# Gate products of a PEER block: the place of their PSUM columns turned round

## Chip, cores and metric

The kernel runs on one core of a Trainium2 chip. The metric is the device time of one execution in microseconds; less is better.

## The reference

Two transformer blocks run one after the other on 256 tokens of width 1024. The first has a short convolution, a latent attention and two SwiGLU layers, the second a chunked attention, an mLSTM and, as its feed-forward part, a PEER layer with 128 x 128 = 16384 experts. Only that layer is touched here:

```python
s_top, i_top = lax.top_k(s, PEER_TOPK)          # 8 heads, two key halves, 16 of 128 each
...
best, ci = lax.top_k(cand, PEER_TOPK)           # 16 of the 16 x 16 sums
e = i1 * N_KEYS + i2
gate = jax.nn.softmax(best, axis=-1)
u = u_exp[e]
v = v_exp[e]
act = jax.nn.gelu(jnp.einsum("thkd,td->thk", u, xb))
return jnp.einsum("thk,thkd->td", (gate * act).astype(xb.dtype), v)
```

Each token has 8 x 16 = 128 chosen experts, each with a gate.

## The kernel before

The kernel gathers no experts. It computes the activation of all 16384 experts for all 256 tokens, multiplies each by the gate (zero where an expert isn't chosen), and sums over all experts. Each fp32 product is made of three products of halves that the faster fp32 format holds (`whi`, `wlo`: high and low half of a weight; `pTh`, `pTl`: of the activations).

- `u_pair(c)` (L1411) takes the c-th of 64 chunks of `peer_u` (1 MB, two rows of 128 experts). ScalarE makes the high half, VectorE the low half (L128, L129), TensorE does 48 products of 256 columns into a bank, and ScalarE writes their GELU to the stash `ST[0]` (chunks 0 to 31) or `ST[1]` (32 to 63) (L1418). A stash holds, for each of 128 partitions (the second key), 64 first keys x 256 tokens in fp32: token neighbours token.
- `weights8(half, t0)` (L1537) makes the gates of 8 tokens and 64 first keys. VectorE compares the indices of the chosen experts with 0 to 127 (`B`, L1551, the second key) and with the 64 first keys of this half (`E`, L1552), and multiplies `E` by the gates, which are cut into three bf16 parts (`Aw`, three instructions of L1555). All of this is in the tile `one`, of which there are 2. For each token TensorE loads `B` (128 choices x 128 second keys) and streams `Aw` (128 choices x 64 first keys), three times, once for each part, into the same 64 columns of a bank: 24 products, each with its weight load. The bank is one of 2 with the tag `mb`. VectorE then multiplies the stash by the bank in place (L1562).
- `v_half` (L1571) multiplies the finished stash, cut into halves by `split` (L135), by the rows of `peer_v`: 12 products of 512 columns for each half chunk, into four banks `acc` that collect over the whole layer.

The order: u chunks 0 to 31; `weights8(0, ...)` for the 32 groups of 8 tokens, among the u chunks 32 to 62; u chunk 63; `weights8(1, ...)` for 32 groups, among the v chunks 0 to 31; v chunks 32 to 63; then residual and final norm. A planner that simulates the engines sets each engine's order; `prio(LOW)` (L1577, L1590) puts the groups behind the chunks, and `prio(-2 * LOW)` (L1557) puts their matmuls ahead of the chunks' again, so that TensorE does them as soon as the masks are planned to be ready. In the order that results, the products of two groups mostly stand together. SP issues the chunks' loads in the order of the code.

Of the kernel before, what the change touches and what calls it, by code (L numbers as in the profile page):

```python
# [16 lines left out]
ALU = mybir.AluOpType  # L17
# [44 lines left out]
def tile_kernel(ctx, tc, A, out, taps=None):  # L62
    nc = tc.nc
# [16 lines left out]
    def mmps(side=None):  # L80

        if side is None:
            turn[0] += 1
            side = turn[0] % turn[1] == 0
        if side:
            return psum.tile([P, 512], F32, name="mb", tag="mb", bufs=2)
        return psum.tile([P, 512], F32, name="mm", tag="mm", bufs=6)
# [4 lines left out]
    @contextmanager  # L92
    def prio(d):

        p = tc.cur_priority
        tc.cur_priority = max(0, p + d)
        try:
            yield
        finally:
            tc.cur_priority = p  # L100
# [44 lines left out]
    def mm(ps, lhsT, rhs, start, stop):  # L145
        nc.tensor.matmul(ps, lhsT, rhs, start=start, stop=stop, skip_group_check=True)  # L146
# [1250 lines left out]
    for c in range(3, 8):  # L1397
        hs = weights[c - 3] if c < 5 else q_halves(c)
        ps = mmps()
# [137 lines left out]
    def weights8(half, t0):  # L1537
        ps = mmps(True)
        n = 8
        one = pk.tile([P, n * 384], BF, name="one", tag="one", bufs=2)  # L1540
        B = one[:, :n * P].rearrange("p (t j) -> p t j", t=n)
        E = one[:, n * P:n * 192]
        Aw = one[:, n * 192:].rearrange("p (i t j) -> p i t j", i=3, t=n)

        def pairs(v, j):
            return v.rearrange("p (t j d) -> p t j d", t=n, d=2) if j is None else v.rearrange("p (j d) -> p j d", d=2)[:, None].to_broadcast([P, n, j, 2])

        def each(v, j):
            return v[:, t0:t0 + n, None, :].to_broadcast([P, n, j, 2])

        nc.vector.tensor_tensor(pairs(one[:, :n * P], None), pairs(iob, 64), each(iT[:, 1], 64), op=ALU.is_equal)  # L1551
        nc.vector.tensor_tensor(pairs(E, None), pairs(iob[:, half * 64:(half + 1) * 64], 32), each(iT[:, 0], 32), op=ALU.is_equal)  # L1552
        for i in range(3):
            o = n * 192 + i * n * 64
            nc.vector.tensor_tensor(pairs(one[:, o:o + n * 64], None), pairs(E, None), each(g3[:, i], 32), op=ALU.mult)  # L1555
        po = ps.rearrange("p (i t) -> p i t", t=n)
        with prio(-2 * LOW):  # L1557
            for t in range(n):
                for i in range(3):
                    mm(po[:, :, t], B[:, t, :], Aw[:, i, t, :], i == 0, i == 2)  # L1560
        v = ST[half][:, :, t0:t0 + n]
        nc.vector.tensor_tensor(v, po, v, op=ALU.mult)  # L1562

    def v_split(c):
        half, o = c // 32, (2 * c) % 64
# [11 lines left out]
    with prio(LOW):  # L1577
        for t0 in range(0, T, 8):
            weights8(0, t0)
# [10 lines left out]
    with prio(LOW):  # L1590
        for t0 in range(0, T, 8):
            weights8(1, t0)
# [31 lines left out]
    for tt in range(NT):  # L1624
        ss = ev[:, 6 * D + 8 * tt:6 * D + 8 * tt + 2]
        for j in range(2):
            o = slice(j * 512, (j + 1) * 512)
            t = rt[tt][:, o]
# [102 lines left out]
```

## Time and profile before

| | us |
|---|---|
| median of 3 runs | 1662.21 (1661.76 to 1663.13) |
| profiled execution | 1662.13 |
| its span, first to last instruction | 1660.4 |
| TensorE (PE) busy | 1637.8 (99%) |
| TensorE weight loads (PEld) | 1515.3 (91%) |
| VectorE (DVE) busy | 1183.4 (71%) |
| ScalarE (ACT) busy | 770.5 (46%) |
| POOL busy | 62.7 (4%) |
| 1536 gate products, sum of their durations | 98.1 |
| 64 products with the stash (L1562), busy time on VectorE | 41.3 |

The granted clock of TensorE is 0.999 of full speed over the span. Matmuls overlap: the sum of their durations is more than the time that they take up, and a start-to-start distance is read from the timeline. Each matmul has two instructions, the load of its stationary operand (PEld) and the product (PE). A line like L146 is that of a helper; tiles tell the groups apart: `mb<-one` are the gate products, `mm<-pT.,w..` the u chunks, `acc<-w..,pT.` the v chunks. The idle time in a group is that of the engine just before its instructions, with what ended it.

### The profile page before, as it was taken

Reading aid. Unit: us, or ns where it says so; the run is one execution under the profiler, and the core shown is the slowest. Engines: PE = TensorE matmul, PEld = TensorE weight load, DVE = VectorE, ACT = ScalarE, POOL = GpSimd, SP = SyncE. Lnnn points to the kernel's source line nnn. Section 1 sums busy time; section 2 is a strip of 40 time slices with the busy share of each in tenths; the row PEclk is TensorE's granted clock in tenths of the full one; section 3 lists DMA queues with packets and bytes.
Section 4 is the critical chain, followed back from the end, with each engine's and each line's share of the span. In section 5 each row is a group of like instructions: output and inputs, shape, how many; then the busy total and the mean of one; then the engine's idle time right before and its main releaser. Section 6 shows DMA issues by size and latency. Waiting matters only on the chain.

```text
span 1660.4 us, 28789 instructions
## 1 busy us (share of the span) xinstructions
PE 1637.8 (99%) x12006; PEld 1515.3 (91%) x12006; DVE 1183.4 (71%) x1925; ACT 770.5 (46%) x1064; POOL 62.7 (4%) x114
## 2 busy tenths in 40 slices
PE   7999999999999999999999999999999999999997
PEld 7999999989999899998999999999999888888886
DVE  5768776666878676766799984877747888755555
ACT  5545444464544466653544444333344333454443
POOL 0000000200000010002000000000000000000001
PEclk9999999999999999999999999999999999999999
DMA  5739665235866455463535545344355434455553
GB/s 225 283 135 349 261 258 220 94 132 218 339 256 242 178 170 176 144 247 130 194 128 180 184 170 181 128 142 137 128 183 212 165 135 155 159 188 201 186 195 127
DMA packets 46274, 312.76 MB, mean 188 GB/s; under 512 B 6240, under 2 KB 6256, under 8 KB 10304
## 3 DMA queue, kind: packets, MB, share of 16 engines
q1 hardware_dynamic: 43344, 300.82, 50.7%
q0 software_dynamic: 2656, 9.06, 1.6%
q8 instruction: 94, 1.54, 0.4%
q10 hardware_dynamic: 144, 1.05, 0.2%
q14 instruction: 36, 0.29, 0.1%
HBM read 308.78 MB, written 2.12 MB: 187 GB/s over the span
## 4 chain that ended last, share of the span: by engine, by line
PE 95%; DVE 2%; DMA 1%; ACT 1%; POOL 0%; issue 0%; SPq 0%; POOLq 0%; DVEq 0%; ACTq 0%
PE mm L146 46%; PE acc L146 32%; PE mb L146 16%; PE mm L217 0%; DMA raw<-in_conv_w_in 0%; DMA raw<-in_mla_w_uq 0%; POOL xn L1219 0%; DVE wlo L129 0%; DVE first L135 0%; ACT pTh L135 0%; PE mb L217 0%; DVE stash L1629 0%; DVE stash L1630 0%; DVE xn L1230 0%; DVE hres L1217 0%
## 5 line engine op out<-in xcount | busy, mean ns | idle before, releaser
L129 DVE TENSOR_TENSOR wlo<-raw,whi 128x1024 fp32r<-128x1024 f32 x492 | 597.7, 1223 | 278.9 <-ACT whi L128 277.8
L128 ACT ACTIVATE whi<-raw 128x1024 fp32r<-128x1024 f32 x492 | 514.6, 1057 | 602.2 <-PE mm L146 360.5
L146 PE MATMUL mm<-pTh,whi 128*128 128x256 f32 x1720 | 489.0, 284 | 0.0
L146 PE MATMUL mm<-pTl,whi 128*128 128x256 f32 x1720 | 487.9, 284 | 0.0
L146 PE MATMUL mm<-pTh,wlo 128*128 128x256 f32 x1720 | 487.2, 284 | 0.0
L146 PEld LDWEIGHTS mm<-pTh,whi 128*128 128x128 f32 x1720 | 329.7, 192 | 1.5 <-issue 0.3
L146 PEld LDWEIGHTS mm<-pTl,whi 128*128 128x128 f32 x1720 | 329.9, 192 | 0.8
L146 PEld LDWEIGHTS mm<-pTh,wlo 128*128 128x128 f32 x1720 | 329.5, 192 | 0.5
L146 PE MATMUL acc<-wlo,pTh 128*128 128x512 f32 x512 | 159.4, 391 | 0.0
L146 PE MATMUL acc<-whi,pTl 128*128 128x512 f32 x512 | 158.3, 389 | 0.0
L146 PE MATMUL acc<-whi,pTh 128*128 128x512 f32 x512 | 145.1, 391 | 0.0
L146 PEld LDWEIGHTS acc<-whi,pTl 128*128 128x128 f32 x512 | 96.1, 188 | 20.1
L146 PEld LDWEIGHTS acc<-whi,pTh 128*128 128x128 f32 x512 | 96.2, 188 | 19.6
L146 PEld LDWEIGHTS acc<-wlo,pTh 128*128 128x128 f32 x512 | 95.6, 189 | 19.1
L146 PE MATMUL mb<-pTh,whi 128*128 128x256 f32 x392 | 111.2, 284 | 0.0
L146 PE MATMUL mb<-pTh,wlo 128*128 128x256 f32 x392 | 110.9, 283 | 0.0
L146 PE MATMUL mb<-pTl,whi 128*128 128x256 f32 x392 | 110.9, 283 | 0.0
L146 PE MATMUL mb<-one 128*128 128x64 bf16 x1536 | 98.1, 246 | 0.0
L146 PEld LDWEIGHTS <-one 128*128 128x128 bf16 x1536 | 87.4, 123 | 6.8 <-DVE wlo L129 2.9
L135 ACT ACTIVATE pTh<-stash 128x512 fp32r<-128x512 f32 x64 | 40.6, 634 | 90.6 <-PE acc L146 89.0
L146 PEld LDWEIGHTS mb<-pTh,whi 128*128 128x128 f32 x392 | 74.8, 191 | 0.6
L146 PEld LDWEIGHTS mb<-pTl,whi 128*128 128x128 f32 x392 | 74.8, 191 | 0.5
(533 smaller groups left out, 2141.5 us busy)
## 6 DMA issues: line engine op xcount, KB each, us to landing
raw<-in_peer_u SPq DMA_DIRECT2D x64, 1024.0 KB, 4.8
raw<-in_peer_v SPq DMA_DIRECT2D x64, 1024.0 KB, 4.8
raw<-in_conv_ffn_w SPq DMA_DIRECT2D x33, 1024.0 KB, 6.8
raw<-in_mla_ffn_w SPq DMA_DIRECT2D x33, 1024.0 KB, 6.8
raw<-in_w_ada SPq DMA_DIRECT2D x24, 1024.0 KB, 8.5
raw<-in_conv_w_in SPq DMA_DIRECT2D x11, 1024.0 KB, 6.4
raw<-in_w_peer_q SPq DMA_DIRECT2D x8, 1024.0 KB, 4.8
raw<-in_conv_w_out SPq DMA_DIRECT2D x4, 1024.0 KB, 11.8
```

The source lines that it names most:

```text
L128: nc.scalar.activation(hi[:, :n], raw[:, a:a + n], AF.Copy)
L129: marks["chunk"] = nc.vector.tensor_sub(lo[:, :n], raw[:, a:a + n], hi[:, :n])
L135: return nc.scalar.activation(hi, src, AF.Copy), nc.vector.tensor_sub(lo, src, hi)
L146: nc.tensor.matmul(ps, lhsT, rhs, start=start, stop=stop, skip_group_check=True)
```

## The change

`po` was a view of the bank in which first key i of token t lies at word 8 i + t: a product wrote 64 words that are 8 words apart, and the bank lay as the stash does. Now first key i of token t lies at word 64 t + i: a product writes 64 neighbouring words, and VectorE's instruction goes through the bank with a step of 64 words (tokens inside, first keys outside), while the stash, read and written, is gone through as before, in runs of 8 tokens. Nothing else changes: the same number of instructions, the same operands and sizes.

```diff
-        po = ps.rearrange("p (i t) -> p i t", t=n)
         with prio(-2 * LOW):
             for t in range(n):
                 for i in range(3):
-                    mm(po[:, :, t], B[:, t, :], Aw[:, i, t, :], i == 0, i == 2)
+                    mm(ps[:, t * 64:(t + 1) * 64], B[:, t, :], Aw[:, i, t, :], i == 0, i == 2)
         v = ST[half][:, :, t0:t0 + n]
-        nc.vector.tensor_tensor(v, po, v, op=ALU.mult)
+        nc.vector.tensor_tensor(v, ps.rearrange("p (t i) -> p i t", t=n), v, op=ALU.mult)
```

## Rows read from the trace of the kernel before

**Rows 1.** The page, parts 1 and 4: busy time, and the chain that ended last.
```profile
PE 1637.8 (99%) x12006; PEld 1515.3 (91%) x12006; DVE 1183.4 (71%) x1925; ACT 770.5 (46%) x1064; POOL 62.7 (4%) x114
...
PE 95%; DVE 2%; DMA 1%; ACT 1%; POOL 0%; issue 0%; SPq 0%; POOLq 0%; DVEq 0%; ACTq 0%
```

**Rows 2.** The page, part 5, and the tile `one`: durations min/median/max in ns.
```profile
L146 PE MATMUL mb<-one 128*128 128x64 bf16 x1536 | 98.1, 246 | 0.0
...
L146 PE MATMUL mb<-one x1536: 229/247/247, 979.2 to 1433.6; 128*128 128x64 bf16 x192
```

**Rows 3.** Timeline of PE (start, us, instruction): three windows closing later and later.
```profile
1269.39 0.29 PE L146 MATMUL mb<-one 128*128 128x64 bf16 x2
...
1269.39 0.34 PE L146 MATMUL mb<-one 128*128 128x64 bf16 x3
...
1269.39 2.85 PE L146 MATMUL mb<-one 128*128 128x64 bf16 x48
```

**Rows 4.** The chain in order of time: start, us, what; v chunks, then u chunks.
```profile
1283.85 8.23 PE acc L146 x36
...
1090.66 7.47 PE mm L146 x62
```

**Rows 5.** Timeline of PEld, two windows: closed behind the first, behind the second load.
```profile
1269.39 0.10 PEld L146 LDWEIGHTS <-one 128*128 128x128 bf16 x1 [0.26 <-issue]
...
1269.39 0.12 PEld L146 LDWEIGHTS <-one 128*128 128x128 bf16 x2 [0.26 <-issue]
```

**Rows 6.** Timeline of PE and PEld, 338.2 to 338.8; a lone fp32 load at 1098.10.
```profile
338.45 0.22 PE L146 MATMUL mm<-trib,identb 128*128 128x128 bf16 x1
338.50 0.44 PE L146 MATMUL mm<-b4h,b4l 128*128 128x128 f32 x2
...
338.45 0.30 PEld L146 LDWEIGHTS mm<-b4h,b4l 128*128 128x128 f32 x2
...
1098.10 0.19 PEld L146 LDWEIGHTS mm<-pTh,whi 128*128 128x128 f32 x1
```

**Rows 7.** Timeline of PE around a gate product that stands alone.
```profile
1097.85 0.28 PE L146 MATMUL mm<-pTl,whi 128*128 128x256 f32 x1
1097.97 0.23 PE L146 MATMUL mb<-one 128*128 128x64 bf16 x1
1098.02 0.36 PE L146 MATMUL mm<-pTh,wlo 128*128 128x256 f32 x1
1098.22 0.28 PE L146 MATMUL mm<-pTh,whi 128*128 128x256 f32 x1
```

**Rows 8.** Single lines on VectorE: durations min/median/max in ns, first and last start.
```profile
L1562 DVE TENSOR_TENSOR stash<-mb,stash x64: 680/686/694, 1033.3 to 1434.5; 128x512 f32<-128x512 f32 x64
...
L1476 DVE TENSOR_TENSOR stash<-stash x2: 625/644/662, 896.3 to 970.2; 128x256 f32<-128x256 bf16 x2
...
L1490 DVE TENSOR_TENSOR stash<-stash x1: 419/419/419, 958.4 to 958.4; 128x256 f32<-128x256 f32 x1
```

**Rows 9.** Busy time by stretch: PE, PEld, DVE, ACT, POOL; clock, DMA share, GB/s.
```profile
1047.56:1191.40 143.84, 143.84 (x1540) 142.08 (x1538) 113.87 (x205) 46.93 (x54) 0.00 (x0) 1.00 0.39 133
1269.39:1431.08 161.69, 161.69 (x1214) 137.19 (x1214) 138.90 (x236) 59.98 (x69) 1.06 (x2) 1.00 0.46 161
```

**Rows 10.** Timeline of DVE in both stretches, and of PE; idle time in brackets.
```profile
1090.64 1.29 DVE L1562 TENSOR_TENSOR stash<-mb,stash 128x512 f32<-128x512 f32 x2 [2.14 <-PE mb L146]
...
1283.83 1.29 DVE L1562 TENSOR_TENSOR stash<-mb,stash 128x512 f32<-128x512 f32 x2 [1.16 <-PE mb L146]
...
1289.06 1.09 DVE L1555 TENSOR_TENSOR one<-one,g 128x512 bf16<-128x512 bf16 x3
...
1291.92 2.85 PE L146 MATMUL mb<-one 128*128 128x64 bf16 x48
```

**Rows 11.** VectorE's groups by line, first 1047.56 to 1191.40, then 1269.39 to 1431.08.
```profile
L1562 DVE TENSOR_TENSOR stash<-mb,stash 128x512 f32<-128x512 f32 x28 | 18.1, 687 | 26.6 <-PE mb L146 26.6
...
L1562 DVE TENSOR_TENSOR stash<-mb,stash 128x512 f32<-128x512 f32 x28 | 18.1, 687 | 14.8 <-PE mb L146 14.8
```

## Prediction

> **What bounds the kernel now.** I began with the page's shares and its chain that ended last: TensorE is busy 99% of the span and carries 95% of the chain, and all three lines of that share are matmuls [rows 1]. So only what shortens the matmul stream, or what makes it wait, moves the end. The costliest groups then show what the change touches: 1536 gate products of 64 columns, each with a weight load of its own [rows 2]. They are few beside the fp32 products, and their mean of 246 ns says little, since matmuls are pipelined; what counts is the step from one start to the next. The timeline gives it. In a window that lets in one, two, three and 48 of them, the run lasts 0.29 us with two, 0.34 with three, 2.85 with 48 [rows 3]; the shortest product, a lone one, lasts 0.229 and most last 0.247 [rows 2], so the first step is about 40 ns and a later one (2.85 - 0.25) / 47 = 55.4 ns. There are 32 such runs (of 44, 46, 47 or 48) and 39 products that stand alone between fp32 products: 1536 - 71 = 1465 steps inside runs, 32 of them first steps, 1433 at 55.4.
>
> **Why a step lasts 55 ns.** This decides the case, and three readings are possible: the columns themselves, the weight load, or the write of each column 8 words from the one before.
> Columns: in the chain's pieces 36 fp32 products of 512 columns pass in 8.23 us (229 ns each) and 62 of 256 columns in 7.47 us (120 ns) [rows 4]. The difference, 108 ns for 256 columns, is 0.42 ns a column; 64 columns are 27 ns, half of what is seen.
> Weight load: when the window closes behind the second load of a run, the two together last 0.12 us where one lasts 0.10 [rows 5], so the second began some 20 ns behind the first, or less. Two fp32 loads in a row last 0.30 us where one lasts 0.19: they follow at 110 ns [rows 6]. So a bf16 load occupies its path for no more than about 20 ns, and from the third on the loads wait for the products.
> Write: the one other bf16 product of the trace, the mask's 128 columns, written to neighbouring words, lasts 0.22 us, and the next product starts 0.05 us behind it, 50 to 60 ns with the rounding of hundredths [rows 6]. The gate product has half its columns and is recorded longer, at 0.23. Something adds one column's time for every column, and what the gate product alone has is the stepped output. I take the write as the cause.
> The Trainium skill, PSUM — Partial Sum Buffer, section Specifications (TRN2), has the same sign: 8-byte cachelines, and any access pattern that isn't contiguous slows matmuls significantly; it gives no price.
>
> **The change, TensorE's side.** Matmuls, loads and their number stay; 64 neighbouring words are written instead of 64 stepped ones. No row shows two 64-column bf16 products at unit step, so the new step is bounded. From below: the mask product's pace, half of its 50 to 60 ns, 28 ns. From above: the line through the two fp32 steps, 229 and 120 ns, meets zero columns at 12 ns, and 27 + 12 = 39 ns, which is also the first step of today's runs [rows 3, 4]. I take 30, nearer to the mask product, since it is the same type with the same kind of load. Saved: 1433 x (55.4 - 30) = 36.4 us, 32 first steps x 10 ns = 0.3, and 32 hand-overs from a run to the fp32 product behind it at 25 ns = 0.8: 37.5 us. At 28 it is 40.5, at 39 it is 24. The 39 lone products give nothing: from one of them the next fp32 product but one starts 0.24 us later (1097.97 to 1098.22) [rows 7], twice the usual 0.12, because the fp32 load behind it has only a short product to hide under; it will be as long.
>
> **VectorE's side.** The product with the stash (64 of them, 686 ns for 512 elements, all near that) [rows 8] keeps its element order: the stash is still read and written in runs of 8 words, as now, and that costs nothing more. New is that each element of the bank lies 64 words from the one before. No row shows a stepped read of PSUM. From below: nothing is added; a gain is excluded, as 686 ns is what any contiguous 512-element fp32 product lasts here. From above: the one VectorE instruction whose inputs both step by 32 bytes (L1476, 16 bf16 elements, in SBUF) lasts 644 ns for 256 elements where a contiguous one lasts 419 [rows 8]: 0.88 ns an element, 0.45 us for 512. With one input stepping instead of two it is between half of that, 0.23, and all, 0.45: I take 0.34, so 1.03 us each and 64 x 0.34 = 22 us of VectorE in all.
> The Trainium skill speaks against the change here: Vector Engine (DVE) Microarchitecture Reference, section 5.2, has full rate only for runs of two adjacent words, and 1.73 ns a column against 1.05 for one source that hops at every element, measured in SBUF. By that the product would be an estimated 0.35 us longer; no row here shows it for PSUM, and the sum would not move.
>
> **Does VectorE's extra lie beside TensorE's work?** I counted in both stretches where runs repeat, 14 runs each. From 1047.56 to 1191.40 (u chunks) VectorE is busy 113.9 of 143.8 us, idle 30.0; from 1269.39 to 1431.08 (v chunks) 138.9 of 161.7, idle 22.8 [rows 9]. Its order in one period: the two products, idle before them until the run ends (1.2 to 2.1 us), then the masks, the weights' low halves between them, and the last gate masks end at 1290.15 for a run that starts at 1291.92, 1.8 us of slack [rows 10]. Most of the idle time is that wait, 26.6 us and 14.8 us [rows 11], and it shrinks by itself when the runs shrink. With 30 ns a run is 1.2 us shorter, so each stretch loses 14 x 1.2 = 17 us, and of VectorE's idle time 13 and 5.8 remain. The 28 products of each add 28 x 0.34 = 9.5. That fits with u chunks and lacks 9.5 - 5.8 = 3.7 us with v chunks, where VectorE then is next: TensorE waits for the masks. I charge the 3.7 in full. At 0.45 the charge is 6.8, at 0 nothing. Behind the product on VectorE stand the next masks and low halves, and the bank goes back to TensorE 0.34 us later; both are inside that count. ScalarE, POOL, SP and the DMAs issue what they did; chunks are asked for a little faster while DMA is busy 39% and 46% there [rows 9].
>
> **Sum.** 37.5 - 3.7 = 33.8 us. The profiled run took 1662.13 us with a span of 1660.4; what lies around the span stays. 1662.1 - 33.8 = 1628 us, and since that run is within 0.1 us of the median of 1662.21, no correction is needed.
>
> **The rivals.**
> A, the hand-over sets the step at 39 ns: for it, the intercept of the fp32 steps; against it, the mask product, whose hand-over leaves next to nothing beyond its columns. Saved 24 us; VectorE has 11 us left for 9.5, so no charge: 1638 us (1639 with a product 0.45 longer).
> B, the change does nothing for TensorE: the pair of load and product, not the write, makes 55 ns. For it: one load per product, and a first step that is shorter than the rest whatever the cause. Against: the loads 20 ns apart. VectorE's 9.5 us fit into 22.8 and 30.0 of idle time, so 1662 us. The Trainium skill has a rule on that side: TensorE: Matmul & The Clock Gate, section Back-to-back issue gap, gives about 81 ns for load and product pairs of 128 columns where a product alone would be 56. An estimate from that, 25 ns above the columns, would leave a 64-column pair at about 54 ns, today's step; the loads' distance in the trace speaks against it.
> C, the stepped read costs VectorE more, 0.6 to 0.9 us: PSUM may be worse than SBUF. The charges are 56 x 0.75 - 18.8 = 23 us in the middle: about 1648 us.
> D, slower: the same read makes VectorE the bound of both stretches. The idle time left is 18.8 us and TensorE's gain there 34 us, so from 52.8 / 56 = 0.94 us more per product (1.63 us each) the change loses. At 1.07 us, each element three ticks instead of one, it loses 7 us: 1669 us. Only a price twice that of the worst row does this.
>
> **How the numbers follow.** Forecast (28 to 34 ns a step, up to 0.45 us more per product): 55%, 1621 to 1634, likeliest 1628. A: 25%, 1634 to 1642. C: 6%, 1641 to 1655. B: 10%, 1659 to 1664. D: 4%. The planner that orders the instructions may shuffle them, which I can't read from a trace; 2 or 3 us either way. The range 1620 to 1645 holds the forecast, A and a part of C, some 8 in 10. What can be told from no change is 0.2%, 3.3 us: faster 0.86 (forecast, A, C), same 0.09, slower 0.05.
>
> **What would show it.** In the new profile a run of 48 should last about 1.65 us instead of 2.85, with the gate product's own duration below the mask product's 0.22. If runs shorten and the time falls by less, the missing part must stand as TensorE waiting for the masks (one) from 1269 on, and the product's duration must tell why. If the runs stay at 2.85 us the step is not the write's, and I am wrong at the root. If the product stays at 0.69 us, the charge falls away and the time is near 1624.

## The result, and the profile after

The changed kernel takes 1622.8 us (median of 4 runs, 1622.62 to 1623.62), the kernel before 1662.18 us (median of 4): ratio 0.9765, 95% interval 0.9753 to 0.9777, 39.4 us less. The profiled execution has a span of 1621.9 us against 1660.4, so 38.5 us show in the traces.

Page of the changed kernel, parts 1 and 4 (busy time; the chain that ended last), as in [rows 1]:

```profile
PE 1599.4 (99%) x12006; PEld 1476.9 (91%) x12006; DVE 1181.9 (73%) x1925; ACT 769.9 (47%) x1064; POOL 62.5 (4%) x114
...
PE 96%; DVE 2%; ACT 1%; DMA 0%; POOL 0%; issue 0%; SPq 0%; POOLq 0%; DVEq 0%
```

TensorE lost 38.4 us of busy time (1637.8 to 1599.4), the whole difference of the spans; VectorE's work is the same within 1.5 us. TensorE's order of instructions is the same in both programs. The loads of the tile `one` in the kernel before (durations min/median/max in ns), then loads and products in the changed kernel, then its timeline of PE in windows that close behind two, three and 48 products, to set beside [rows 2, 3]:

```profile
L146 PEld LDWEIGHTS <-one x1536: 95/125/125, 979.2 to 1433.6; 128*128 128x128 bf16 x192
...
L146 PEld LDWEIGHTS <-one x1536: 95/98/100, 979.5 to 1395.1; 128*128 128x128 bf16 x192
L146 PE MATMUL mb<-one x1536: 193/193/203, 979.5 to 1395.2; 128*128 128x64 bf16 x192
```

```profile
1269.37 0.23 PE L146 MATMUL mb<-one 128*128 128x64 bf16 x2
...
1269.37 0.26 PE L146 MATMUL mb<-one 128*128 128x64 bf16 x3
...
1269.37 1.57 PE L146 MATMUL mb<-one 128*128 128x64 bf16 x48
```

A run of 48 lasts 1.57 us instead of 2.85. One step is (1.57 - 0.193) / 47 = 29.3 ns; it was 55.4. Both are means over a run with its first step of some 40 ns in them; the later steps alone go from (2.85 - 0.34) / 45 = 55.8 ns to (1.57 - 0.26) / 45 = 29.1. The 26.7 ns between them are 0.42 ns for each of the 64 columns, as much as a column takes in the fp32 products [rows 4]. This time of one column is called a tick below. A gate product is 193 ns long where it was 229 to 247, now below the mask product's 0.22 us, and a weight load is recorded at 98 ns where most took 125.

VectorE's product with the stash (its line moved up by one), and the two stretches where runs repeat, 14 of them in each; busy time of PE, PEld, DVE, ACT, POOL, as in [rows 8, 9]:

```profile
L1561 DVE TENSOR_TENSOR stash<-mb,stash x64: 678/682/693, 1032.5 to 1396.5; 128x512 f32<-128x512 f32 x64
```

```profile
1045.45:1172.49 127.04, 127.04 (x1539) 125.26 (x1538) 113.64 (x205) 46.87 (x54) 0.00 (x0) 1.00 0.44 150
1249.29:1393.81 144.52, 144.52 (x1215) 119.72 (x1214) 138.20 (x236) 59.89 (x69) 1.05 (x2) 1.00 0.52 180
```

The stepped read is free: 682 ns against 686. The stretches are 16.8 and 17.2 us shorter, and TensorE is still without a gap in both. VectorE's busy time in them is what it was (113.6 and 138.2), so its idle time fell from 30.0 and 22.8 us to 13.4 and 6.3. Where it went is seen in the groups by line, first u, then v chunks, as in [rows 11]:

```profile
L1561 DVE TENSOR_TENSOR stash<-mb,stash 128x512 f32<-128x512 f32 x28 | 18.1, 685 | 10.0 <-PE mb L146 10.0
...
L1561 DVE TENSOR_TENSOR stash<-mb,stash 128x512 f32<-128x512 f32 x28 | 18.0, 683 | 0.2
```

VectorE's idle time before this product, its wait for the run's end, went from 26.6 to 10.0 us and from 14.8 to 0.2: the shorter run gives that time back.

### The profile page after: what moved, and what is told of

Its sections match the earlier page's. It is cut to its first block, busy times and chain, and to the rows that moved or that the text cites. A ratio compares the mean times of both kernels' runs of the same rounds, so it can differ in the third digit from the quotient of the medians.

```text
span 1621.9 us, 28789 instructions
## 1 busy us (share of the span) xinstructions
PE 1599.4 (99%) x12006; PEld 1476.9 (91%) x12006; DVE 1181.9 (73%) x1925; ACT 769.9 (47%) x1064; POOL 62.5 (4%) x114
## 4 chain that ended last, share of the span: by engine, by line
PE 96%; DVE 2%; ACT 1%; DMA 0%; POOL 0%; issue 0%; SPq 0%; POOLq 0%; DVEq 0%
PE mm L146 48%; PE acc L146 33%; PE mb L146 14%; PE mm L217 1%; DMA raw<-in_conv_w_in 0%; POOL xn L1219 0%; PE mb L217 0%; DVE first L135 0%; DVE stash L1628 0%; DVE stash L1629 0%; ACT pTh L135 0%; DVE wlo L129 0%; DVE xn L1230 0%; DVE hres L1217 0%; ACT b4h L566 0%
## 5 line engine op out<-in xcount | busy, mean ns | idle before, releaser
L146 PEld LDWEIGHTS mb<-pTh,wlo 128*128 128x128 f32 x392 | 74.8, 191 | 0.0
L1555 DVE TENSOR_TENSOR one<-one,g 128x512 bf16<-128x512 bf16 x192 | 68.7, 416 | 0.0
```

## Experiments

The theory: a column that isn't written next to the one before it costs TensorE a second tick (0.42 ns more), and nothing else of the change matters. Steps in this section are means over a run, as above. Rivals: the step is set by the pair of load and product (B of the prediction), by the distance, or partly by VectorE's side.

**One part alone.** Old write, new read:

```diff
-                    mm(ps[:, t * 64:(t + 1) * 64], B[:, t, :], Aw[:, i, t, :], i == 0, i == 2)
+                    mm(ps.rearrange("p (i t) -> p i t", t=n)[:, :, t], B[:, t, :], Aw[:, i, t, :], i == 0, i == 2)
```

> One part alone: products write 8 words apart as in the kernel before, VectorE reads the bank with a step of 64 words as in the changed one (so the gates of a group meet the wrong experts and tokens; the work is the same). Theory (all of the gain is TensorE's step, the stepped read costs nothing): step 55.5 ns, VectorE's product 0.68 to 0.69 us, time 1661 to 1663 us. Rival (the order of the read or the planner's other order on VectorE brings a part of the gain): 1640 to 1658 us. Rival (the stepped read costs something that the changed kernel hides): above 1664 us or a product above 0.75 us.

Measured: 1661.84 us, ratio 0.9998 (0.9989 to 1.0008). Tile `one` and the product's line of this kernel, and a run of 46 in its timeline:

```profile
L146 PE MATMUL mb<-one x1536: 229/247/247, 979.0 to 1433.4; 128*128 128x64 bf16 x192
...
L1561 DVE TENSOR_TENSOR stash<-mb,stash x64: 678/682/693, 1033.1 to 1434.2; 128x512 f32<-128x512 f32 x64
...
1047.32 2.74 PE L146 MATMUL mb<-one 128*128 128x64 bf16 x46
```

The step is back, (2.74 - 0.247) / 45 = 55.4 ns, and so is the time, with VectorE's order of instructions exactly that of the changed kernel. The gain is the write's alone, and the stepped read by itself costs nothing: 682 ns.

**How near is near enough?** First a step of 2 words, two tokens interleaved. Here and in the two runs with 32 columns only TensorE's line is shown; VectorE's line, which reads the bank as it then lies, is left out.

```diff
-                    mm(ps[:, t * 64:(t + 1) * 64], ...
+                    mm(ps.rearrange("p (a i b) -> p a i b", a=n // 2, b=2)[:, t // 2, :, t % 2], ...
```

> The product writes 64 words 2 words apart (two tokens interleaved), VectorE reads the bank accordingly; nothing else differs from the changed kernel. Theory (a column costs a second tick as soon as it isn't the direct neighbour of the one before it, however near it lies): step 55 ns in a run, a run of 48 products 2.85 us in the timeline, gate product 0.23 to 0.247 us long, time 1661 to 1663 us. Rival (the cost comes with the distance, and 2 words are still near): step between 29 and 45 ns, time 1623 to 1645 us.

Measured: 1661.89 us, ratio 0.9999 (0.9988 to 1.0009). Then pairs of neighbours, 16 words from pair to pair:

```diff
-                    mm(ps[:, t * 64:(t + 1) * 64], B[:, t, :], Aw[:, i, t, :], ...
+                    mm(ps.rearrange("p (j t d) -> p t j d", t=n, d=2)[:, t], B[:, t, :],
+                       Aw[:, i, t, :].rearrange("p (j d) -> p j d", d=2), ...
```

> The product writes pairs of neighbouring words, 16 words from pair to pair; VectorE reads the bank accordingly (step 2 inside, so each element on its own). Theory, finer form (two neighbours suffice for the full rate, any hop between pairs is free): step 29.3 ns, a run of 48 in 1.57 us, time 1622 to 1624 us. Rival (only an output at unit step throughout is fast, every hop costs something): 32 hops in place of 64, step 42 ns, time about 1642 us; or no difference from the stepped output, 55 ns, 1662 us.

Measured: 1623.3 us, ratio 0.9767 (0.9751 to 0.9783). In both kernels the products' order and VectorE's 0.68 us are those of the changed kernel. Tile `one` and a run of 46, step 2 first, then pairs:

```profile
L146 PE MATMUL mb<-one x1536: 229/247/247, 978.9 to 1433.3; 128*128 128x64 bf16 x192
...
1047.27 2.74 PE L146 MATMUL mb<-one 128*128 128x64 bf16 x46
```

```profile
L146 PE MATMUL mb<-one x1536: 193/193/203, 979.2 to 1394.9; 128*128 128x64 bf16 x192
...
1045.19 1.51 PE L146 MATMUL mb<-one 128*128 128x64 bf16 x46
```

A step of 2 words costs as much as one of 8 (55.4 ns); pairs 64 bytes apart cost nothing ((1.51 - 0.193) / 45 = 29.3 ns). So it is not the distance, and it is not the hop: it is whether two columns in a row fill neighbouring words, 8 bytes. Every pair here begins at an even word; pairs that begin at an odd one were not tried. Eight bytes is the cacheline that the Trainium skill, PSUM — Partial Sum Buffer, section Specifications (TRN2), gives for PSUM; its wording there, that any access pattern that isn't contiguous slows matmuls, is stricter than what is measured here.

**A second tick per column, or a fixed cost per product?** 32 of the 64 columns, 8 words apart:

```diff
-                    mm(ps[:, t * 64:(t + 1) * 64], B[:, t, :], Aw[:, i, t, :], ...
+                    mm(ps.rearrange("p (i t) -> p i t", t=n)[:, :32, t], B[:, t, :], Aw[:, i, t, :32], ...
```

> Each gate product streams 32 of its 64 columns, written 8 words apart (the gates of the other 32 first keys are left out; VectorE reads the 32 twice). Theory (a second tick for each stepped column): 32 x 2 x 0.42 + 2.5, step 29 to 30 ns, time near 1623 us. Rival (a stepped output costs a product a fixed 26 ns): step 42 ns or more, time near 1642 us.

And 32 columns side by side:

```diff
-                    mm(ps[:, t * 64:(t + 1) * 64], B[:, t, :], Aw[:, i, t, :], ...
+                    mm(ps[:, t * 64:t * 64 + 32], B[:, t, :], Aw[:, i, t, :32], ...
```

> What bounds the step next: each gate product streams only 32 of its 64 columns, to neighbouring words (the gates of the other 32 first keys are left out; VectorE reads the 32 twice, so its work stays). Theory (columns alone set the step of 29.3 ns: 0.42 ns a column and 2.5 ns): step 16 ns. Rival (load, issue or hand-over have a floor near 29 ns, which the columns only happen to meet): step 25 to 29 ns. In time, 19 us less at 16 ns, if VectorE, idle 6.3 us of 144.5 among the v chunks, lets it: 1604 to 1614 us; with the floor 1618 to 1623 us.

Measured, one time each: 1624.58 us stepped, 1618.27 us side by side. Tile `one` and a run of 46 in the timeline, stepped first:

```profile
L146 PE MATMUL mb<-one x1536: 193/193/203, 979.4 to 1401.8; 128*128 128x32 bf16 x192
...
1053.64 1.51 PE L146 MATMUL mb<-one 128*128 128x32 bf16 x46
```

```profile
L146 PE MATMUL mb<-one x1536: 176/176/190, 978.9 to 1395.5; 128*128 128x32 bf16 x192
...
1052.52 1.32 PE L146 MATMUL mb<-one 128*128 128x32 bf16 x46
```

32 stepped columns take (1.51 - 0.193) / 45 = 29.3 ns a step and 193 ns a product, just what 64 neighbours take: a stepped column is two ticks. The second run is a miss of the theory: 32 neighbours step at (1.32 - 0.176) / 45 = 25.4 ns, not at 16, so the rival was right that a floor lies just below. With 64 columns the changed kernel is 4 ns above it. Whether the load, the issue or the hand-over makes this floor was not tried. Both runs also bury B: with the same loads the step is 55.4, 29.3 or 25.4 ns by the number and the place of the columns. (The planner broke some runs of these two kernels in two, so their times are not compared to the microsecond.)

**VectorE's price, made real.** The stash, not the bank, is gone through with a hop:

```diff
-        nc.vector.tensor_tensor(v, ps.rearrange("p (t i) -> p i t", t=n), v, op=ALU.mult)
+        nc.vector.tensor_tensor(v.rearrange("p i t -> p t i"), ps.rearrange("p (t i) -> p t i", t=n),
+                                v.rearrange("p i t -> p t i"), op=ALU.mult)
```

> VectorE goes through the bank in the order in which it lies, and through the stash, in SBUF, with a step of 256 words for every element, read and write; TensorE's part is that of the changed kernel. Theory (a hop at every element is free in PSUM but costs in SBUF): from the 644 ns instruction, 0.88 ns an element at most, the product lasts 0.9 to 1.15 us. Then VectorE becomes the bound among the v chunks, where it is idle 6.3 us of 144.5 in the changed kernel, and just fits among the u chunks (13.4 us idle): 28 x 0.4 - 6.3 = 5 us lost, time 1625 to 1632 us. Rival (hops cost nothing in this instruction, wherever they lie): 0.68 us, 1622 to 1624 us. Rival C of the prediction in full (0.6 to 0.9 us more): 1640 to 1655 us.

Measured: 1637.41 us, ratio 0.9852 (0.9837 to 0.9867), 14.6 us slower than the changed kernel. The product's line, the two stretches with the same instructions of TensorE as in the changed kernel (columns as before), and TensorE's gate products among the v chunks with the idle time before them:

```profile
L1561 DVE TENSOR_TENSOR stash<-mb,stash x64: 1308/1343/1398, 1032.4 to 1412.1; 128x512 f32<-128x512 f32 x64
...
1045.41:1175.23 129.82, 129.17 (x1539) 126.21 (x1537) 129.82 (x205) 46.96 (x54) 0.00 (x0) 1.00 0.43 147
1252.46:1406.81 154.35, 148.96 (x1214) 121.47 (x1214) 152.86 (x235) 61.40 (x68) 1.06 (x2) 1.00 0.49 167
...
L146 PE MATMUL mb<-one 128*128 128x64 bf16 x673 | 27.5, 193 | 5.4 <-DVE one L1555 3.1
```

The hop in SBUF, in the read and in the write of the stash together, costs 1343 - 682 = 661 ns, 1.29 ns an element: more than the 0.2 to 0.45 us that was expected from the instruction of [rows 8], so that expectation missed, in size and in time. Which of the two costs how much was not tried. What follows from it was right: VectorE is busy 129.8 of 129.8 and 152.9 of 154.4 us, and TensorE waits for the masks, with 5.4 us of idle time before its gate products among the v chunks. The prediction's rule, 28 x 0.66 less the idle time left (13.4 and 6.3 us), gives 5.1 + 12.2 = 17 us for the two stretches; they grew by 2.8 and 9.8, together 12.6 us. VectorE's busy time in them grew by 16.2 and 14.7 us and not by 28 x 0.66 = 18.5 in each; why by less was not worked out.

**A version that beats both.** A group's first product used to be ready one mask early, and the planner then put it alone between fp32 products ([rows 7]). In the changed kernel too, 0.24 us pass from it to the next product but one:

```profile
1089.87 0.20 PE L146 MATMUL mb<-one 128*128 128x64 bf16 x1
1089.91 0.36 PE L146 MATMUL mm<-pTh,wlo 128*128 128x256 f32 x1
1090.11 0.28 PE L146 MATMUL mm<-pTh,whi 128*128 128x256 f32 x1
```

Start with the last part:

```diff
-                for i in range(3):
-                    mm(ps[:, t * 64:(t + 1) * 64], B[:, t, :], Aw[:, i, t, :], i == 0, i == 2)
+                for i in (2, 0, 1):
+                    mm(ps[:, t * 64:(t + 1) * 64], B[:, t, :], Aw[:, i, t, :], i == 2, i == 1)
```

> A version that may beat both: the three gate parts of a token are multiplied in the order last, first, second (only the order of the sum changes), so the first product of a group waits for the last mask, the planner no longer puts single products between fp32 products, and all 1536 stand in 32 runs of 48. Theory (a lone product costs 120 ns, since the fp32 load behind it lies bare, against 29 in a run): 39 x 0.091 = 3.5 us less than the changed kernel, 1619.3 us, ratio to the kernel before 0.974. Rival (the run starts later and VectorE's wait for it or TensorE's for the masks takes that back): within 1 us of 1622.8 us.

Measured: 1619.64 us (5 runs, 1619.22 to 1620.27), ratio to the kernel before 0.9746 (0.9732 to 0.9759), 3.2 us below the changed kernel, whose runs do not overlap with these. The chain of this kernel among the u chunks (start, us, what), and the same place in the changed one:

```profile
1052.82 1.42 PE mb L146 x48
1054.24 7.86 PE mm L146 x65
1062.10 1.42 PE mb L146 x48
```

```profile
1052.91 0.05 PE mb L146
1052.95 0.31 PE mm L146 x2
1053.27 0.05 PE mb L146
1053.31 0.31 PE mm L146 x2
1053.63 1.36 PE mb L146 x46
1054.98 7.50 PE mm L146 x62
```

Two fp32 products behind a lone one last 0.31 us where two of 65 last 0.24. All 1536 now stand in 32 runs of 48, and nothing took the gain back: 39 x 0.091 = 3.5 us were expected.

## Why the prediction was right, and where it was off

- *What bounds*: right. TensorE has no gap in either stretch, before or after, and its saving is the saving.
- *Why a step lasts 55 ns*: right, and now shown: one part alone, 2 words, pairs, and 32 stepped columns all agree with the second tick.
- *The new step*: 30 ns taken, 29.1 measured. The 55.4 ns of today's step was a little short, since the first step of 40 ns is in that mean; without it a later step goes from 55.8 to 29.1 ns, and 1433 x 26.7 = 38.3 us instead of 36.4. The mask product was the right row to be nearest to. The bound from above was built on two rows that mean something else: the first step of a run stays at 0.23 - 0.193 = 0.04 us with neighbouring words, so it is not the write's and not a hand-over that every product pays. Hence rival A fell, and the 0.3 us for first steps did not come. The hand-overs from a run to the fp32 product went from 56 to 29 ns, 0.9 us for 32 of them, as charged. Together that is 39.1 us, and the traces show 38.5; some 0.4 of the difference stand before any matmul, as TensorE's first product starts at 8.4 us instead of 8.0. The medians show 39.4, because the profiled execution of the changed kernel is the slowest of its four (1623.62 us, against a median of 1622.8).
- *Lone products*: right that they give nothing: still 0.24 us to the next but one.
- *VectorE's product*: the step that failed. 0.34 us were put on it and none came. The row that set the bound hops in SBUF, and the change hops in PSUM; the run with the hop in the stash shows that hops in SBUF are as dear as feared, and dearer, while the one in PSUM is free. This is the charge of 3.7 us, most of the 5.2 us between 1628 and 1622.8. The prediction had named this outcome among its signs: with the product still at 0.69 us the time was to be near 1624.
- *VectorE's cover*: right. 13 and 5.8 us of idle time were to remain, 13.4 and 6.3 did, and the wait for the run's end shrank by itself.
- *Rivals*: B is refuted. The Trainium skill's rate for pairs of load and product (TensorE: Matmul & The Clock Gate, section Back-to-back issue gap), from which some 54 ns were estimated, does not hold for these pairs: 29.3 ns. The Trainium skill, same page, section "Wait — 56ns, not 53.3ns?", has a floor of about 25 ns from start to start. The trace agrees: 25.4 ns with 32 columns. C did not happen, but with 0.66 us more per product, forced on purpose, the mechanism came, at some three quarters of the rule's price (17 us by the rule, 12.6 in the two stretches). D was not reached; its sum takes only TensorE's gain in the two stretches, 34 us, where that of C takes all 37.5.

## What to carry to other kernels

Lay a matmul's output so that at least two columns in a row fill neighbouring words, and put the transposing step on the engine that reads the bank: VectorE's stepped read of PSUM cost nothing here, while hops in SBUF, in a read and in the write, doubled the instruction. A stepped output costs by the column: it nearly doubled the step of products of 64 columns (29.3 to 55.4 ns), and added only 3.9 ns to products of 32, where the floor of 25.4 ns covers most of it. Other widths were not tried. Before charging a hop, look at which memory the row that prices it comes from, and ask whether the cover remains once the stream it lies under gets shorter.

## What the runs show of the hardware

- PSUM takes a stepped output at full rate if it comes in pairs of words: pairs 64 bytes apart step at 29.3 ns, as neighbours do, while single words only 8 bytes apart cost the full second tick (55.4 ns).
- VectorE reads PSUM at a step of 64 words at 682 ns for 512 elements, the contiguous rate; with one input and the output hopping 256 words in SBUF it takes 1343 ns.
- Bf16 pairs of weight load and product follow at 25.4 ns with 32 columns, where the columns alone would take some 13; with 64 columns they follow at 29.3. So 64 columns cost little more than 32. What holds the shorter ones back was not tried.
- The first step of a run is 0.04 us with the stepped output and with neighbouring words alike, shorter than the later steps of 55.8 ns and longer than those of 29.1. Why was not tried.
